# The queue that issues the stores of the gated output: Pool's in place of SyncE's

## The chip, the cores and the metric

The program runs on one core of a Trainium2 chip. The metric is the device time of one execution in microseconds, as the median of several. Before the change three executions took 2771.98, 2772.40 and 2774.57 us, so the median is 2772.4 us.

The engines are named as in the profile: PE is TensorE's matmul and PEld its weight load, DVE is VectorE, ACT is ScalarE, POOL is GpSimd and SP is SyncE, which in this kernel does nothing but issue DMAs. SPq is SP's queue of such issues.

## The reference, cut to what matters

One layer (DEPTH = 1) of a backbone with width 1024 works on 2048 latent tokens and 128 context tokens: a bidirectional gated recurrence (HGRN2), then a feed-forward block with a short convolution, then a final norm. The change touches the feed-forward block alone:

```python
def conv_ffn(h, w_up, conv_w, conv_b, w_down, grid_axis):
    a, g = jnp.split(h @ w_up, 2, axis=-1)
    a = token_conv(a, conv_w, conv_b, grid_axis)
    return (jax.nn.silu(a) * g) @ w_down
...
xp = xp + mod_p[5] * conv_ffn(hp, ffn_w_up[l], ffn_conv_w[l], ffn_conv_b[l], ffn_w_down[l], None)
xs = xs + mod_s[5] * conv_ffn(hs, ffn_w_up[l], ffn_conv_w[l], ffn_conv_b[l], ffn_w_down[l], 2)
```

The inner width (D_FF) is 2816, so `h @ w_up` gives 5632 columns: 2816 for `a`, which is convolved over three neighbours in a row of 64 latent tokens (or in the 128 context tokens), and 2816 for the gate `g`.

## The kernel before

**Operands.** Every f32 operand of a matmul is kept as two f16 tiles, a high part and a remainder, and a product is three matmuls (high by high, high by low, low by high). The high part is written by ACT and the remainder by DVE (`split`, L970 and L971; for weights `part`, L1037 and L1038 in the up stage, L1232 and L1233 in the down stage).

**Pieces.** The latent tokens go in four pieces of 512 (p = 0 to 3), the context is a fifth piece (CTX) of 128. The 2816 inner columns are 22 blocks of 128 and are taken two at a time (`cb` = 0, 2, ..., 20), so there are 11 periods of the up stage. One period makes, for p = 0 to 3, `up(cb, p)`, and after p = 1 also `up_ctx(cb)` for the context.

**Up stage.** A product of a 2x2 block of weights with a 2x2 block of tokens takes seven partial products (Strassen and Winograd's scheme) in the order 1, 2, 6, 5, 7, 3, 4. `product` issues twelve matmuls for one of them into a bank (L1076) and evacuates it: by ACT where it writes a quarter of the result (L1085, L1089, L1091, L1097), by DVE where it adds to one (L1082). Two such sets run side by side, one for `a` and one for `g`.

**Weights of the up stage.** `quad(cb, i)` loads the raw f32 weights `r` of two column blocks (L1043, two loads of 512 KB; i = 0 for `a`, i = 1 for `g`), forms the four sums `s` on DVE (L1048 to L1051) and splits the eight operands into `w` (L1037 and L1038). The two quads of the next period are put on a list (`pending`) after `up_ctx`, and steps of them are handed out between products (`post`).

**Gated output.** When `up(cb, p)` has its result, `gate(cb, p)` is put on another list: it convolves `a` (ACT L1103, DVE L1110 and L1112), applies silu (ACT L1137), multiplies by the gate (DVE L1139), forms the four sums `t` of the tokens' quarters (DVE L1147 to L1151), and splits all seven operands of the down stage into the tile `u` (L970 and L971). `u` is then stored to DRAM, in `UD[p]` (L1158): 896 KB, 1792 rows of 512 B, once for each of 11 x 4 latent pieces. `gate_ctx` does the same for the 128 context tokens without sums and stores 64 KB into `UC` (L1191), 22 times.

**Down stage.** `load_rd` brings raw weights `rawd` (L1228, 704 KB each), `part` splits them into `wd`, `sums_down` makes sums of them (L1244 to L1248), `load_uc` and `load_ut` read the stored outputs back as `U` (L1270, L1289), `load_xd` the residual `x` (L1264). `down_ctx` multiplies for the context (L416 to L418, added to `x` at L1283), `down` for the latent pieces (L1307, added at L1316). `final_norm` ends a piece; its power function is on Pool (L344). The first loads of `rawd` and their splitting fall into the last period of the up stage.

**Order.** The code states what each engine does; a scheduler puts the instructions of each engine into a fixed order at build time, with the help of its own estimate of durations, and each engine then runs them in order and waits where an operand isn't ready. Before the change every DMA of the kernel is issued by SP, in one order. Tiles live in SBUF at places given out by `place`, which reuses the place of a tile whose last reader has come: a load into a tile waits for whatever still reads what lay there before, and a store is such a reader until it has landed.

Of the kernel before, what the change touches and what calls it, by code (L numbers as in the profile page):

```python
# [214 lines left out]
def stages(nc, tl, pt, drt, xT, adaH, adaT, pvec, w_in, w_out, w_up, w_down, state, yT, st_out):  # L215
# [752 lines left out]
    def split(dst, src, scale=None):  # L968

        A.activation(dst[0], src, AF.Copy)  # L970
        V.tensor_tensor(dst[1], src, dst[0], ALU.subtract)  # L971
# [127 lines left out]
    def conv(cols, p, n):  # L1099


        for cb, y, a in cols:
            A.activation(y, a, AF.Identity, bias=pv[:, PV_CB + cb : PV_CB + cb + 1],  # L1103
                         scale=cws[:, 22 + cb : 23 + cb])
        yield
        row = ROW if p != CTX else n
        for cb, y, a in cols:
            y3 = y.rearrange("p (r c) -> p r c", c=row)
            a3 = a.rearrange("p (r c) -> p r c", c=row)
            V.scalar_tensor_tensor(y3[:, :, 1:], a3[:, :, : row - 1], cws[:, cb : cb + 1],  # L1110
                                   y3[:, :, 1:], ALU.mult, ALU.add)
            V.scalar_tensor_tensor(y3[:, :, : row - 1], a3[:, :, 1:], cws[:, 44 + cb : 45 + cb],  # L1112
                                   y3[:, :, : row - 1], ALU.mult, ALU.add)
        yield
# [4 lines left out]
    UD = {p: drt([P, 7, 2, NCB // 2, HN], F16, f"ud{p}") for p in range(CTX)}  # L1119
    UC = drt([P, NCB, 2, NCTX], F16, "uc")  # L1120
# [11 lines left out]
    def gate(cb, p, qa, qg):  # L1132
        y = tl([P, 2, 2, HN], F32, "y")
        flat = y.rearrange("p j h c -> p (j h c)")
        yield from conv([(cb + j, flat[:, 512 * j : 512 * j + 512], qa["out"][j])
                         for j in range(2)], p, 512)
        A.activation(flat, flat, AF.Silu)  # L1137
        yield
        V.tensor_tensor(flat, flat, qg["tile"], ALU.mult)  # L1139
        yield  # L1140
        u = tl([P, 7, 2, HN], F16, "u")

        def part(z, src):
            split((u[:, z : z + 2, 0], u[:, z : z + 2, 1]), src)

        t13 = tl([P, 2, HN], F32, "t")
        V.tensor_tensor(t13[:, 0], y[:, 0, 1], y[:, 0, 0], ALU.subtract)  # L1147
        V.tensor_tensor(t13[:, 1], y[:, 1, 1], y[:, 0, 1], ALU.subtract)
        t24 = tl([P, 2, HN], F32, "t")
        V.tensor_tensor(t24[:, 0], y[:, 1, 1], t13[:, 0], ALU.subtract)  # L1150
        V.tensor_tensor(t24[:, 1], y[:, 1, 0], t24[:, 0], ALU.subtract)  # L1151
        part(0, y[:, :, 0])
        split((u[:, 6, 0], u[:, 6, 1]), y[:, 1, 1])
        yield
        part(2, t13)
        yield
        part(4, t24)
        nc.sync.dma_start(UD[p][:, :, :, cb // 2], u)  # L1158

    def up(cb, p):  # L1160
        qs = []
        for i, s in enumerate((1.0, IWS)):
            t = tl([P, 2 * 512], F32, "c7")
            qs.append({"scale": s, "tile": t,
                       "out": [t[:, 512 * j : 512 * j + 512] for j in range(2)]})
        for i in (1, 2, 6, 5, 7, 3, 4):
            while any(PROD[i][0] not in WQ.get((cb, j), {}) for j in range(2)):
                post()
            for j in range(2):
                product(qs[j], i, WQ[cb, j], TT[p])  # L1170
            post()
            tick()
            if i == 6 and cb + 2 == NCB and p + 1 == CTX:
                load_uc()
                load_ut(0, "B11")
                for j in range(2):
                    load_xd(CTX, j, 0, NCTX)
                load_xd(0, 0, 0)
        gates.append(gate(cb, p, *qs))

    def gate_ctx(cb, a, g):
        n = NCTX
        y = tl([P, n], F32, "y")
        yield from conv([(cb, y, a)], CTX, n)
        A.activation(y, y, AF.Silu)
        yield
        V.tensor_tensor(y, y, g, ALU.mult)
        u = tl([P, 2, n], F16, "u")
        yield
        split((u[:, 0], u[:, 1]), y)  # L1190
        nc.sync.dma_start(UC[:, cb], u)  # L1191

    def up_ctx(cb):
        n = NCTX
        for j in range(2):
            pa, pg = pt([P, 512], "pj"), pt([P, 512], "pj")
            for pp, i in ((pa, 0), (pg, 1)):
                for k in range(KT):
                    wt = WQ[cb, i][("A11", "A12", "A21", "A22")[2 * j + k // 4]]
                    ks = slice(k % 4 * P, k % 4 * P + P)  # L1200
                    mm3(pp[:, :n], (wt[:, 0, ks], wt[:, 1, ks]), TT[CTX][:, :, k], n,
                        k == 0, k == KT - 1)
            a, g = tl([P, n], F32, "y"), tl([P, n], F32, "y")
            A.activation(a, pa[:, :n], AF.Copy)
            A.activation(g, pg[:, :n], AF.Copy, scale=IWS)
            pending.append(gate_ctx(cb + j, a, g))
            post()
# [268 lines left out]
```

## Time and profile before

| | before |
|---|---|
| median of three executions | 2772.4 us |
| the profiled execution | 2777.14 us |
| its span on the core | 2775.2 us |
| mean granted clock of TensorE | 0.993 |
| the up stage's periods in the trace | about 1430 to 2325 us |
| ud stores (L1158) | 44 of 896 KB, median 4.8 us from issue to landing |
| uc stores (L1191) | 22 of 64 KB, median 1.5 us |
| r loads (L1043) | 44 of 512 KB, median 4.0 us |
| rawd loads (L1228) | 20 of 704 KB, median 8.1 us |
| U loads from ud (L1289) | 56 of 704 KB, median 4.9 us |

The span runs from the first to the last instruction in the trace. The time of the profiled execution is 1.9 us longer than that, and 4.7 us above the median. In the rows of the profile an instruction has its engine, its line in the kernel, its operation and its tiles, written as out<-in. In a timeline the start comes first and the duration second; the bracket at the end tells how long the engine idled before it, and what ended this. In a table of waits a row has the engine and the line that waited, what it waited for, and then the sum in us, the number of waits and the longest one.

### The profile page before, as it was taken

The page shows a single profiled execution, that of the slowest core. Times are in us where ns is not written, and L with a number is a line of the kernel's source. Part 1 is how long each engine was busy: PE and PEld are TensorE (multiplying, and loading weights), DVE is VectorE, ACT ScalarE, POOL GpSimd, SP SyncE. Part 2 cuts the span into 40 slices and gives each one's busy share as a digit, 9 for nine tenths or more (in the row PEclk, how much of TensorE's full clock was granted, in tenths as well). Part 3 has the DMA queues.
Part 4 walks back from the last instruction along what each step waited for, and adds up shares of the span by engine and source line. Part 5 has one row for each costly group of instructions (what it writes and reads, how often), then busy time and mean ns, then how long its engine had stood idle before and what let it go on. Part 6 is the DMA issues. An engine that isn't in the chain of part 4 may idle for free.

```text
span 2775.2 us, 57195 instructions
## 1 busy us (share of the span) xinstructions
PE 2705.4 (97%) x23576; PEld 2129.1 (77%) x23576; DVE 1886.0 (68%) x5324; ACT 1071.8 (39%) x2373; POOL 72.9 (3%) x84
## 2 busy tenths in 40 slices
PE   8999999999999999999999999999999999999998
PEld 4677777777777677765578888888888988888887
DVE  7887887887876766755996767666677677623123
ACT  5533334343434242513664545445455453300000
POOL 0100000000000000000000000000000000000000
PEclk9999999999999999999999999999999999999999
DMA  7011213121201010345112232221212275344352
GB/s 265 27 63 42 70 34 95 32 74 39 73 6 54 6 54 4 110 137 194 67 41 85 63 89 67 73 86 56 86 58 77 77 200 170 127 156 137 123 166 73
DMA packets 194005, 239.73 MB, mean 86 GB/s; under 512 B 12368, under 2 KB 148432, under 8 KB 193744
## 3 DMA queue, kind: packets, MB, share of 16 engines
q1 hardware_dynamic: 193744, 236.08, 26.9%
q8 instruction: 185, 3.03, 0.5%
q14 instruction: 76, 0.62, 0.1%
HBM read 166.44 MB, written 69.60 MB: 85 GB/s over the span
## 4 chain that ended last, share of the span: by engine, by line
PE 58%; DVE 16%; DMA 5%; ACT 2%; issue 2%; POOL 0%; SPq 0%; DVEq 0%; POOLq 0%; ACTq 0%
PE pj_p L1307 11%; PE pj_p L1076 9%; PE sc_p L1076 6%; PE pj_p L418 5%; PE pj_p L416 5%; PE pj_p L417 5%; DMA r<-w_up 3%; PE pj_p L539 3%; PE pj_p L538 3%; PE pj_p L540 3%; DMA ud<-u 2%; DVE u L971 2%; PE sc_p L1307 1%; PE sc_p L692 1%; DVE wd L1233 1%
## 5 line engine op out<-in xcount | busy, mean ns | idle before, releaser
L1076 PEld LDWEIGHTS <-w 128*128 128x128 f16 x7392 | 725.0, 98 | 115.4 <-issue 29.7
L1076 PE MATMUL pj_p<-T,w 128*128 128x256 f16 x4224 | 491.0, 274 | 24.2 <-DVE c L1082 16.4
L1307 PEld LDWEIGHTS <-wd 128*128 128x128 f16 x3696 | 361.5, 98 | 53.5 <-issue 8.8
L1076 PE MATMUL sc_p<-T,w 128*128 128x256 f16 x3168 | 367.8, 273 | 0.0
L1307 PE MATMUL pj_p<-U,wd 128*128 128x256 f16 x3168 | 354.3, 273 | 5.7 <-DVE x L1316 5.7
L416 PE MATMUL pj_p<-H,wp 128*128 128x512 f16 x768 | 291.2, 380 | 2.8 <-ACT H L395 2.4
L417 PE MATMUL pj_p<-H,wp 128*128 128x512 f16 x768 | 292.6, 381 | 0.5 <-DVE H L400 0.4
L418 PE MATMUL pj_p<-H,wp 128*128 128x512 f16 x768 | 292.3, 381 | 0.0
L540 PE MATMUL pj_p<-wp,H 128*128 128x256 f16 x1024 | 279.1, 273 | 0.0
L538 PE MATMUL pj_p<-wp,H 128*128 128x256 f16 x1024 | 279.1, 273 | 0.0
L539 PE MATMUL pj_p<-wp,H 128*128 128x256 f16 x1024 | 279.1, 273 | 0.0
L1316 DVE SCALAR_TENSOR_TENSOR x<-pj_p,g,x 128x256 f32<-128x256 f32 x96 | 46.4, 483 | 211.6 <-PE pj_p L1307 211.5
L418 PEld LDWEIGHTS <-wp 128*128 128x128 f16 x960 | 94.2, 98 | 91.4 <-issue 2.6
L416 PEld LDWEIGHTS <-wp 128*128 128x128 f16 x960 | 94.3, 98 | 83.5 <-issue 4.2
L417 PEld LDWEIGHTS <-wp 128*128 128x128 f16 x960 | 94.2, 98 | 81.1 <-issue 2.0
L363 ACT ACTIVATE n<-x 128x256 f32<-128x256 f32 (+1 forms) x63 | 25.0, 403 | 262.9 <-DVE x L1316 201.9
L1103 ACT ACTIVATE y<-c,pv,cws 128x512 f32<-128x512 f32 x88 | 71.2, 811 | 137.1 <-DVE c L1082 133.9
L511 ACT ACTIVATE f<-pj_p 128x512 f32<-128x512 f32 x64 | 38.0, 596 | 185.2 <-PE pj_p L418 185.1
L539 PEld LDWEIGHTS <-H 128*128 128x128 f16 x1024 | 100.2, 98 | 11.8
L540 PEld LDWEIGHTS <-H 128*128 128x128 f16 x1024 | 100.2, 98 | 11.7
L538 PEld LDWEIGHTS <-H 128*128 128x128 f16 x1024 | 100.3, 98 | 11.5
L417 PE MATMUL pj_p<-og,wo 128*128 128x512 f16 (+1 forms) x320 | 108.9, 349 | 0.0
(281 smaller groups left out, 5037.6 us busy)
## 6 DMA issues: line engine op xcount, KB each, us to landing
ud<-u SPq DMA_DIRECT2D x44, 896.0 KB, 4.8
U<-ud SPq DMA_DIRECT2D x56, 704.0 KB, 4.9
r<-w_up SPq DMA_DIRECT2D x44, 512.0 KB, 4.0
wr<-w_in SPq DMA_DIRECT2D x40, 512.0 KB, 4.2
wr<-adaT SPq DMA_DIRECT2D x32, 512.0 KB, 3.7
rawd<-w_down SPq DMA_DIRECT2D x20, 704.0 KB, 8.1
x<-xT SPq DMA_DIRECT2D x32, 256.0 KB, 5.3
sp<-oT SPq DMA_DIRECT2D x32, 256.0 KB, 2.2
```

The source lines that it names most:

```text
L416: T.matmul(out, whl[0], hhl[:, 0, :n], start=first, stop=False)
L417: T.matmul(out, whl[0], hhl[:, 1, :n], start=False, stop=False)
L418: T.matmul(out, whl[1], hhl[:, 0, :n], start=False, stop=last)
L511: A.activation(ft, pj[:, :n], AF.Tanh, scale=0.5 * IWS)
L538: T.matmul(o, hp[k][:, 0, tok], wvg[0][:, k], start=(k == 0), stop=False)
L539: T.matmul(o, hp[k][:, 0, tok], wvg[1][:, k], start=False, stop=False)
L540: T.matmul(o, hp[k][:, 1, tok], wvg[0][:, k], start=False, stop=(k == KT - 1))
L971: V.tensor_tensor(dst[1], src, dst[0], ALU.subtract)
L1076: T.matmul(out, wt[:, a, ks], tt[:, b, k], start=first and k == 0 and n == 0, stop=i in (2, 3, 4) and k == 3 and n == 2, skip_group_check= ...
L1103: A.activation(y, a, AF.Identity, bias=pv[:, PV_CB + cb : PV_CB + cb + 1], scale=cws[:, 22 + cb : 23 + cb])
L1307: T.matmul(out, w[:, a, k], UT[p, zb][b][:, k], start=first and i % 2 == 0 and k == 0 and q == 0, stop=n in (2, 3, 4) and k == KP - 1 and ...
L1316: V.scalar_tensor_tensor(x, get(src), g64[:, 1, m, 0:1], x, ALU.mult, ALU.add)
```

## The change

The two stores of the gated output are issued by Pool's queue instead of SP's. Nothing else in the code differs:

```diff
@@ gate @@
         part(4, t24)
-        nc.sync.dma_start(UD[p][:, :, :, cb // 2], u)
+        nc.gpsimd.dma_start(UD[p][:, :, :, cb // 2], u)
...
@@ gate_ctx @@
         split((u[:, 0], u[:, 1]), y)
-        nc.sync.dma_start(UC[:, cb], u)
+        nc.gpsimd.dma_start(UC[:, cb], u)
```

SP then has 489 rows in its program in place of 555, and Pool 155 in place of 89. Loads stay with SP. The tiles keep their places in SBUF. As the scheduler's estimate changes with the queue, some instructions of DVE and ACT change places too; the rows below show it at three places, `-` for before and `+` for the change. In a row stand the line, the operation, out<-in with the numbers of the tiles, and the shape.

SP in the up stage, from the first period on: between loads of raw weights (`r`) stood the stores of a gated latent piece (`ud`) and of the gated context (`uc`).

```order
 L1043 DMA r_18298<-w_up 128x1024
-L1158 DMA ud_15452<-u_17998 1792x1x256
 L1043 DMA r_18300<-w_up 128x1024
-L1191 DMA uc<-u_18187 128x256
-L1191 DMA uc<-u_18257 128x256
-L1158 DMA ud_15453<-u_18284 1792x1x256
 L1043 DMA r_18478<-w_up 128x1024
 L1043 DMA r_18480<-w_up 128x1024
-L1158 DMA ud_15454<-u_18622 1792x1x256
-L1158 DMA ud_15455<-u_18843 1792x1x256
 L1043 DMA r_19358<-w_up 128x1024
```

The loads keep their order and follow one another; the same stores stand in Pool's program in the same order, after the last of its small instructions for the norms (L344) and with nothing between them.

DVE in one of the periods of the up stage, when the second quad of the next period comes in: `r_22718` and `r_22720` are its two raw blocks, `s_...` the four sums, `c_2572` and `c_2573` the results that are being evacuated from the banks `pj` and `sc`.

```order
+L1050 TENSOR_TENSOR s_22724<-r_22718,r_22720 128x512
 L1048 TENSOR_TENSOR s_22722<-r_22720 128x512
+L1049 TENSOR_TENSOR s_22723<-s_22722,r_22718 128x512
+L1051 TENSOR_TENSOR s_22725<-r_22718,s_22723 128x512
 L1082 SCALAR_TENSOR_TENSOR c_2572_22428<-pj_p_22430,c_2572_22428 128x256
-L1049 TENSOR_TENSOR s_22723<-s_22722,r_22718 128x512
-L1050 TENSOR_TENSOR s_22724<-r_22718,r_22720 128x512
 L1082 SCALAR_TENSOR_TENSOR c_2573_22429<-pj_p_22444,c_2573_22429 128x256
-L1051 TENSOR_TENSOR s_22725<-r_22718,s_22723 128x512
 L1082 SCALAR_TENSOR_TENSOR c_2572_22428<-sc_p_22550,c_2572_22428 128x256
```

One sum stood ahead of the first evacuation, now all four do. The same holds in four more periods, with the quads 20598, 23778, 24838 and 25898, where two, three, one and three sums stood ahead of it.

ACT in the last period, where the up stage goes over into the down stage: `wd_...` are the high parts of the down weights made from `rawd_...`, `c_2944` and `c_2945` results of the up stage's last products but one, and `u_28881` a context store's tile.

```order
+L1232 ACTIVATE wd_28925<-rawd_28453 128x1408
 L1085 ACTIVATE c_2945_28813<-pj_p_28828 128x256
 L970 ACTIVATE u_28881<-y_28846 128x128
+L1232 ACTIVATE wd_28993<-rawd_28796 128x1408
 L1089 ACTIVATE c_2944_28812<-pj_p_28814 128x256
-L1232 ACTIVATE wd_28925<-rawd_28453 128x1408
+L1232 ACTIVATE wd_28996<-rawd_28798 128x1408
 L1089 ACTIVATE c_2945_28813<-pj_p_28828 128x256
+L1232 ACTIVATE wd_28922<-rawd_28451 128x1408
 L1091 ACTIVATE c_2944_28812<-sc_p_28928 128x256
-L1232 ACTIVATE wd_28993<-rawd_28796 128x1408
-L1232 ACTIVATE wd_28922<-rawd_28451 128x1408
```

Three of the splittings L1232 stand one to three places earlier than before: `wd_28925` ahead of an L1085, `wd_28993` (into the place that the `u` of piece 1 has left) and `wd_28996` ahead of an L1089.

## The prediction

> **What bounds the kernel now.** I begin with the page: the shares of the engines, then a table by stretches of time for the part of the program that the stores stand in, then PE's waits in it.
>
> ```profile
> PE 2705.4 (97%) x23576; PEld 2129.1 (77%) x23576; DVE 1886.0 (68%) x5324; ACT 1071.8 (39%) x2373; POOL 72.9 (3%) x84
> 1430.00:2250.00 820.00, 799.72 (x7723) 716.71 (x7721) 573.10 (x1101) 410.58 (x872) 0.00 (x0) 1.00 0.27 78
> 2250.00:2330.00 80.00, 71.76 (x817) 65.39 (x815) 68.42 (x91) 39.26 (x61) 0.00 (x0) 0.94 0.70 204
> ```
>
> The last two rows give, for a stretch, its length and the busy time of PE, PEld, DVE, ACT and POOL, then granted clock, DMA share and GB/s. PE is the bound. In the up stage it idles for 820.00 − 799.72 = 20.3 us, and in the 80 us in which the up stage goes over into the down stage for 80.00 − 71.76 = 8.2 us. The DMA engines are 27% busy and POOL does nothing at all, so neither is short of time; a store matters only where somebody waits for it, or for a load behind it. The waits in the up stage:
>
> ```profile
> PE pj_p L1076 <- DVE c L1082: 15.5, 13, 2.6
> PE pj_p L1076 <- ACT c L1085: 2.4, 6, 0.6
> PE pj_p L1076 <- ACT c L1089: 1.1, 1, 1.1
> PE pj_p L1076 <- ACT y L1204: 1.0, 4, 0.4
> SPq L1043 <- DMA ud<-u: 62.3, 15, 4.4
> ACT w L1037 <- DMA r<-w_up: 59.5, 14, 7.2
> DVE s L1048 <- DMA r<-w_up: 33.1, 8, 5.0
> ```
>
> PE is never held by a DMA itself, only by evacuations on DVE and ACT that stand in order behind an instruction which waits for a load of raw weights `r`. And 15 times such a load was itself waiting for a **store to land** (the SPq row), because the tile `r` takes memory that a `u` still being stored holds. SP is idle then: its order costs nothing at these places, only the store's landing does. One of them, on SP, ACT and PE:
>
> ```profile
> 1754.99 0.51 SPq L1158 DMA_DIRECT2D ud<-u  x1
> 1759.85 1.85 SPq L1043 DMA_DIRECT2D r<-w_up  x2
> 1764.15 0.63 ACT L1037 ACTIVATE w<-r 128x512 f16<-128x512 f32 x1 [6.48 <-DMA r<-w_up]
> 1770.65 0.49 PE L1076 MATMUL pj_p<-T,w 128*128 128x256 f16 x3 [0.18 <-ACT y L1204]
> ```
>
> The store begins at 1754.99; 4.86 us later the load starts, 4.3 us after that ACT, and ACT's later work holds PE for 0.18 us. Whatever the store lands later, PE waits longer.
>
> **The change, term by term.** 44 stores of 896 KB and 22 of 64 KB leave SP's queue for Pool's. SP issues 66 instructions fewer, which by itself saves nothing, as SP has slack. Pool has none of its own work in the up stage. The bytes stay, the tiles and their memory stay.
>
> ```profile
> L1158 SPq DMA_DIRECT2D ud<-u x44: 513/519/767, 1445.0 to 2342.2; - x44
> DMA to landing us min/median/max: 4.8/4.8/6.8
> L344 POOL TENSOR_TENSOR rs<-rs,mh 128x4 f32<-128x4 f32 (+2 forms) x19 | 21.7, 1144 | 1567.6 <-DVE rs L342 1567.6
> ```
>
> *Unknown price Δ: how much later than now a store lands if Pool issues it.* No DMA of the trace is issued by Pool. Lower end: Pool is as prompt as SP, Δ = 0 (0.52 us for the issue, 4.8 to the landing); nothing shows a store that undercuts 4.8, so I don't go below. Upper end: the slowest landing of these stores, 6.8 − 4.8 = +2.0. A near row is the smallest work that Pool does, 1.144 us for 128x4 numbers against SP's 0.52, +0.6. I take the middle of +0.6 and +2.0, **Δ = +1.3**, since a store of 1792 rows is more than that instruction. (The Trainium skill, "DMA: Bandwidth & Descriptors", section "Latency and other measured facts", gives a first byte after about 1 us from Pool and 0.6 from SP; an estimate of Δ = +0.4 by that page would make the next term +3.2 and the whole sum −3.8. No run here shows it.)
>
> *Loads that wait for a landing.* Of the 15, followed to PE one by one, 8 end in a wait of PE (0.18 to 1.14 us now, at 1477.5, 1509.6, 1521.3, 1545.5, 1609.3, 1770.6, 1937.5, 2100.4); these have no slack, and pay Δ in full. Three more of them:
>
> ```profile
> 1477.53 2.67 PE L1076 MATMUL pj_p<-T,w 128*128 128x256 f16 x23 [1.14 <-ACT c L1089]
> 1520.26 0.69 DVE L1050 TENSOR_TENSOR s<-r,r 128x512 f32<-128x512 f32 x1 [4.02 <-DMA ud<-u]
> 2100.42 0.49 PE L1076 MATMUL pj_p<-T,w 128*128 128x256 f16 x3 [0.26 <-ACT y L1204]
> 1657.54 0.51 SPq L1158 DMA_DIRECT2D ud<-u  x1
> 1662.37 0.34 SPq L1043 DMA_DIRECT2D r<-w_up  x1
> 1665.75 4.53 PE L1076 MATMUL pj_p<-T,w 128*128 128x256 f16 x40
> 1670.12 2.78 PE L1076 MATMUL sc_p<-T,w 128*128 128x256 f16 x24
> ```
>
> The other 7 are like that of 1662.37: the load waits too, but PE runs on without a gap; they have some 1.5 to 2 us of slack by the same following. Term: 8 × 1.3 = **+10.4** (0 to +16 between the ends).
>
> *Loads that stand behind a store in SP's queue.* In five periods the last `r` of the next block's weights is issued right behind a store, and shares the queue with it:
>
> ```profile
> 1780.40 0.52 SPq L1158 DMA_DIRECT2D ud<-u  x1
> 1781.33 1.74 SPq L1043 DMA_DIRECT2D r<-w_up  x1
> r<-w_up SPq DMA_DIRECT2D x1, 512.0 KB, 3.7
> r<-w_up SPq DMA_DIRECT2D x1, 512.0 KB, 7.3
> 1788.76 0.69 DVE L1048 TENSOR_TENSOR s<-r 128x512 f32<-128x512 f32 x1 [5.04 <-DMA r<-w_up]
> 1789.37 0.42 DVE L1082 SCALAR_TENSOR_TENSOR c<-pj_p,c 128x256 f32<-128x256 f32 x1
> 1789.84 5.41 PE L1076 MATMUL pj_p<-T,w 128*128 128x256 f16 x32 [2.63 <-DVE c L1082]
> ```
>
> The `r` ahead of the store lands in 3.7 us, the one behind it in 7.3 (the two DMA rows, of the windows 1779:1781 and 1781:1790), and PE loses 2.63 us. With the store in another queue the second should land between 3.7 and 7.3 us after its issue: 0 to 3.6 us earlier, I take the middle, 1.8. But the new program order on DVE takes half of it back. Of the four sums (0.61 us from start to start: 1788.76 to 1789.37) more stand ahead of the evacuation L1082 than before: 4 instead of 2, 1, 3, 1 and 3 in the five periods, 10 more in all, 6.1 us. Term: 6.1 − 5 × 1.8 = **−3** (from 6.1 − 18 = −12 to +6). That PE waits longer than 2.6 us here also halves its clock for a moment (32 matmuls in 5.41 us above, where 48 take 5.40 elsewhere: 1.8 us); that goes or stays with the wait, inside these ends.
>
> *The transition.* Here SP really holds the stores up, behind loads whose issue is slow:
>
> ```profile
> 2252.43 15.61 SPq L1228 DMA_DIRECT2D rawd<-w_down  x6
> 2268.13 2.36 SPq L1191 DMA_DIRECT2D uc<-u  x1
> 2270.60 0.52 SPq L1158 DMA_DIRECT2D ud<-u  x1
> 2263.76 0.68 DVE L971 TENSOR_TENSOR u<-t,u 128x512 f16<-128x512 f32 x1
> 2274.22 1.38 ACT L1232 ACTIVATE wd<-rawd 128x1408 f16<-128x1408 f32 x1 [6.04 <-DMA uc<-u]
> 2275.63 1.63 DVE L1233 SCALAR_TENSOR_TENSOR wd<-rawd,wd 128x1408 f16<-128x1408 f32 x1 [6.38 <-ACT wd L1232]
> PE pj_p L1076 <- ACT c L1089: 2.9, 1, 2.9
> PE pj_p L418 <- DVE wd L1233: 3.7, 1, 3.7
> ```
>
> The `u` was whole at 2264.44 (end of the DVE row), its store left at 2270.60. Pool would issue it some 6 us sooner, beside loads that fill the DMA engines. ACT waits 6.04 and DVE 6.38 us; of the shortfall PE pays 2.9 us at once and 1.6 + 3.7 us at 2321 to 2327, when DVE has been full since 2275. Against it stands ACT's new order: the L1232 that reuses the large `u` now comes ahead of the L1089 that PE needs. It waits for a landing at 2264.4 + 4.8 + Δ = 2270.5 if nothing hinders it, 6 us later if the loads do (now it lands in 6.0). Term: the best is all of 2.9 + 5.3 and as much again of halved clock, about −14; the worst is L1089 3 us later than now, +3. I take **−4**, as the loads still fill the engines there.
>
> **Sum**: 10.4 − 3 − 4 = +3.4 us. The profiled execution took 2777.1 us (span 2775.2), 4.7 over the median 2772.4; +3.4 makes 2780.5 of it, or **2776** against the median. After the up stage I count nothing: the last store leaves at 2342 and POOL's next instruction comes at 2356.3.
>
> **Rivals.** *A: Pool is slow with 1792 rows.* If writing the packets' list takes Pool longer than the engines take to move them, Δ goes past 2. Against it: POOL's L344 does its work in 1.1 us. For it: the 1792 rows of 512 B are many, and SP already takes 0.52 us instead of the 0.33 of an `r`. From Δ = 2 the other 7 places lose their slack too, and waits of PE over 2.6 us cost 1.8 us of clock each. At Δ = 2.5: 8 × 2.5 + 7 × 0.7 + 8 × 1.8 − 7 = +32, **2805**; at 4.5 (the delay that an uc store, 1.5 us, has at worst, 6.0): 36 + 19 + 15 − 7 = +63, 2835. A related mechanism is that a busy DVE (573.10 of 820 us) holds Pool's writing of that list up, by an instruction at a time; its price is bounded by the two above. The Trainium skill, "SBUF — State Buffer", section "Who interferes with whom", has that for copies, casts and tensor-by-scalar operations of DVE, not for two-tensor ones; the DVE rows above are all of two tensors, so by that page this does not happen here.
>
> ```profile
> DMA to landing us min/median/max: 1.5/1.5/6.0
> ```
>
> *B: the gains win.* Δ at most 0.3: 8 × 0.2 = +1.6, the second `r` lands 2.5 us sooner (6.1 − 12.5 = −6) and the transition gives −7: −11, **2761**. For it: 7.3 against 3.7 us, and 6 us of queueing that the rows show. Against it: DVE's and ACT's new orders.
>
> *C: nothing moves.* The stores use the same 16 engines, and if they are served in the same turn, all landings stay; the new orders then cost and bring about nothing: **2772**.
>
> **How the numbers follow.** The forecast (Δ from 0.6 to 2, sum −8 to +18) has a chance of 0.47: 0.08 faster, 0.25 same, 0.14 slower, each by over 0.2% (5.5 us, about what a measurement of this kernel can tell from none). A 0.25, all slower. B 0.18, all faster. C 0.10, same. Together faster 0.26, same 0.35, slower 0.39. The forecast's own range is 2764 to 2790; the whole range takes in B and most of A, 2758 to 2825.
>
> **What would show it.** The landing of L1158 in the changed profile gives Δ: near 6.1 for the forecast, 4.8 for B, over 6.8 for A. The gaps at the eight places should each have grown by Δ; the second `r` should land in under 7.3 us, yet DVE's L1082 start about as late as now; the 6.04 and 6.38 us waits at 2268 to 2276 should be shorter. Wrong would be: ud landings under 4.8 us, `r` loads slowed by sharing the engines with a store at places that have no store behind them now, or a PE gap at the places with slack.

## The result, and the profile after

The changed kernel takes 2807.85 us (median of 4, 2806.36 to 2810.33) against 2773.49 us for the kernel before, run beside it: a ratio of 1.0124 with a 95% interval of 1.0111 to 1.0137, so 34.4 us slower. The profiled execution took 2810.33 us with a span of 2808.3, against 2777.14 and 2775.2 before.

From the page of the changed kernel, the engines, the new queue beside the old one, and the landing times:

```profile
PE 2717.3 (97%) x23576; PEld 2134.5 (76%) x23576; DVE 1889.3 (67%) x5324; ACT 1072.3 (38%) x2373; POOL 131.4 (5%) x150
q1 hardware_dynamic: 111024, 194.26, 21.0%
q0 software_dynamic: 11264, 41.82, 4.8%
ud<-u POOLq DMA_DIRECT2D x44, 896.0 KB, 5.5
r<-w_up SPq DMA_DIRECT2D x44, 512.0 KB, 3.6
```

POOL's busy time grew by the 66 issues, and queue q0 now carries their bytes. PE does the same 23576 matmuls, yet is busy 2717.3 − 2705.4 = 11.9 us longer. That is time at a lower clock: the stretches in which the granted clock is 0.5 add up to 64.0 us in this trace and to 40.8 in that of before, and half of the difference is 11.6 us. So of the 33 us in the span about a third is clock and two thirds are waits. The waits of PE in the up stage (from 1430 to 2300 us), and those that the stores end:

```profile
PE pj_p L1076 <- DVE c L1082: 29.6, 11, 5.0
PE pj_p L1076 <- ACT c L1085: 6.5, 10, 2.2
PE pj_p L1076 <- ACT y L1204: 2.6, 4, 0.8
PE pj_p L1076 <- ACT c L1089: 0.3, 1, 0.3
  DVE s L1048: 5.0, 5
  DVE s L1050: 4.7, 1
DMA to landing us min/median/max: 5.4/5.5/9.6
```

The first row has doubled (15.5 before), and its longest wait is 5.0 instead of 2.6. The two DVE rows are from the view of line L1158, which says who waited for its stores: DVE's sums L1048 now do, five times; before they did not appear there at all. The landings have a median of 5.5 us from Pool's start and a longest of 9.6, against 4.8 and 6.8.

**Where in the program.** The start of every 168th matmul of L1076 marks a piece, 44 in the up stage, four to a period. (In the trace of before these matmuls run from 1396.1 to 2302.8 us, not from about 1430 to 2325, as the table of times at the start has it.) Cutting both traces there, and adding up what the pieces of a kind take longer than before, gives this (us; worked out from the matmul rows of the profiled executions, which themselves differ by several us between executions of one kernel):

```
                 periods 1-9,      periods 1-9,      period 10   after the last   all, to PE's
                 pieces 0 and 1    pieces 2 and 3                L1076            last matmul
after                +4.7              +22.5            +3.5          +1.9           +32.9
p1_pool              +1.5              +19.4            +3.1          -0.1           +23.3
p1_sp                +5.2               +5.0            +1.9          +3.2           +13.0
p1_act               -0.1               +9.4            +1.1          +0.3           +10.2
order_pool           +4.9               +7.9            +2.7          +3.3           +19.0
late_pool            +6.4              -17.7            +2.7          +2.5            -6.3
late_sp              -0.5              -18.9            +1.3          +1.0           -18.1
uc_pool              -1.3               -5.0            +1.3          -1.2            -6.3
last_pool            -1.4               -3.6            +2.3          +4.4            +1.1
```

The last column also holds what lies ahead of period 1. The row of uc_pool, whose median is that of the kernel before, shows how far one trace can be off: −5.0 in one column. Part of that is clock: the trace of before has two stretches of 3.41 us at half clock in these pieces, each a loss of 1.7 us, and that of uc_pool has none. So differences of a few us in the table decide nothing. The loads that wait for a landing (pieces 0 and 1) cost little. Two thirds of the loss sit in pieces 2 and 3, nearly all of it in piece 2, where the second quad of the next block comes in. One such place, in period 6. Before, from the timelines of SP, DVE and PE:

```profile
1947.26 0.52 SPq L1158 DMA_DIRECT2D ud<-u  x1
1948.20 0.35 SPq L1043 DMA_DIRECT2D r<-w_up  x1
1954.94 0.69 DVE L1048 TENSOR_TENSOR s<-r 128x512 f32<-128x512 f32 x1 [4.36 <-DMA r<-w_up]
1955.55 0.42 DVE L1082 SCALAR_TENSOR_TENSOR c<-pj_p,c 128x256 f32<-128x256 f32 x1
1956.02 5.62 PE L1076 MATMUL pj_p<-T,w 128*128 128x256 f16 x48 [1.95 <-DVE c L1082]
```

After, from those of SP, POOL, DVE and PE:

```profile
1960.37 2.16 SPq L1043 DMA_DIRECT2D r<-w_up  x2
1961.78 1.06 POOL L1158 DMA_DIRECT2D ud<-u  x1 [1.85 <-DVE u L971]
1968.02 0.69 DVE L1050 TENSOR_TENSOR s<-r,r 128x512 f32<-128x512 f32 x1 [3.44 <-issue]
1970.15 0.69 DVE L1048 TENSOR_TENSOR s<-r 128x512 f32<-128x512 f32 x1 [1.43 <-DMA ud<-u]
1972.21 0.75 DVE L1082 SCALAR_TENSOR_TENSOR c<-pj_p,c 128x256 f32<-128x256 f32 x2
1972.68 8.30 PE L1076 MATMUL pj_p<-T,w 128*128 128x256 f16 x48 [4.61 <-DVE c L1082]
```

Read these from below. PE waits 4.61 us instead of 1.95 and then runs its 48 matmuls in 8.30 us, which take 5.40 at full clock. It waited for an evacuation L1082, which stood on DVE behind four sums instead of one. The first of them, L1050, needs both raw blocks, and they are there by 1968.0 (the second lands at 1967.94). The next, L1048, could start at once if it only needed `r`; it waits 1.43 us more **for the store to land**, because its tile `s` takes the memory of the `u` that is being stored. It lands at 1970.12. The sum needed the landing before too: there the store stood ahead of the load in SP's queue and landed at 1953.61, the load at 1954.86, so the load's landing hid it, and the profile put the wait down to the load alone. It is the same in all five periods in which DVE's order changed: before, the store landed 1.2 to 2.3 us ahead of the second load; after, it lands 1.5 to 2.2 us behind it (from the landings in the two traces).

### The profile page after: what moved, and what is told of

It reads as the page before. It is cut to its first block, busy times and chain, and to the rows that moved or that the text cites. A ratio compares the mean times of both kernels' runs of the same rounds, so it can differ in the third digit from the quotient of the medians.

```text
span 2808.3 us, 57270 instructions
## 1 busy us (share of the span) xinstructions
PE 2717.3 (97%) x23576; PEld 2134.5 (76%) x23576; DVE 1889.3 (67%) x5324; ACT 1072.3 (38%) x2373; POOL 131.4 (5%) x150
## 3 DMA queue, kind: packets, MB, share of 16 engines
q1 hardware_dynamic: 111024, 194.26, 21.0%
q0 software_dynamic: 11264, 41.82, 4.8%
## 4 chain that ended last, share of the span: by engine, by line
PE 42%; issue 28%; DVE 9%; DMA 2%; POOL 2%; ACT 1%; POOLq 0%; SPq 0%; DVEq 0%; ACTq 0%
PE pj_p L1307 11%; PE pj_p L418 5%; PE pj_p L416 5%; PE pj_p L417 5%; PE pj_p L539 3%; PE pj_p L538 3%; PE pj_p L540 3%; DMA ud<-u 1%; PE sc_p L1307 1%; PE sc_p L692 1%; POOL ud L1158 1%; PE sc_p L652 1%; PE sc_p L661 1%; DVE x L1330 1%; DVE T L971 1%
## 5 line engine op out<-in xcount | busy, mean ns | idle before, releaser
L1076 PEld LDWEIGHTS <-w 128*128 128x128 f16 x7392 | 730.0, 99 | 141.7 <-issue 50.9
L1076 PE MATMUL pj_p<-T,w 128*128 128x256 f16 x4224 | 499.9, 277 | 44.6 <-DVE c L1082 30.5
L1076 PE MATMUL sc_p<-T,w 128*128 128x256 f16 x3168 | 369.1, 273 | 0.1
```

The costliest lines, as they stand in the source:

```text
L1076: T.matmul(out, wt[:, a, ks], tt[:, b, k], start=first and k == 0 and n == 0, stop=i in (2, 3, 4) and k == 3 and n == 2, skip_group_check= ...
```

## The experiments

All times are medians, beside runs of the kernel before on the same chip (2773.2 us with the first four, 2773.3 with the others). The first three are about which stores bring the loss, and which queue.

**Piece 1's stores alone on Pool** (p1_pool):

```diff
-        nc.sync.dma_start(UD[p][:, :, :, cb // 2], u)
+        (nc.gpsimd if p == 1 else nc.sync).dma_start(UD[p][:, :, :, cb // 2], u)
```

> Only the stores of piece 1 (11 of 44) go to Pool, all else stays with SP. Theory 1: the loss sits where the sums s (or raw blocks r) of the next block's second quad take the memory of the piece-1 output that is still being stored, and the evacuations L1082 stand behind those sums on DVE; then nearly all of the 34 us is here: 2772 + 22 to 26, so 2794 to 2798 us, with the third piece of most periods 1 to 5 us longer than before. Theory 2 (every Pool store pays about 1.2 us where a load waits for its landing, as the forecast had it): the first pairs wait for piece-0 stores, which stay with SP, so 2770 to 2776.

It took 2798.55 us, a ratio of 1.0091 (1.0068 to 1.0114). Eleven of the 66 stores bring 25 us, almost all in pieces 2 and 3. In the same trace, the two kinds of stores land side by side (issues by queue), and DVE's sums wait for them (from the view of line L1158):

```profile
ud<-u SPq DMA_DIRECT2D x33, 896.0 KB, 4.8
ud<-u POOLq DMA_DIRECT2D x11, 896.0 KB, 7.8
  DVE s L1048: 8.7, 6
```

That is half a microsecond above the range of theory 1, which is right about these stores. The forecast's reading, that they cost next to nothing, is not.

**All others on Pool, piece 1 on SP** (p1_sp): the same line with `p == 1` going to `nc.sync` and the rest to `nc.gpsimd`, and the context stores on Pool.

> The counterpart: the stores of pieces 0, 2, 3 and of the context go to Pool, piece 1 stays with SP. Theory 1: what is left is the first pairs, 0.3 to 0.6 us each and 2.5 once, 5 to 9 us in all: 2777 to 2782. Theory 2: eight places at 1.2 us and the odd ones in part: 2782 to 2800.

It took 2790.06 us, 1.0057 (1.0038 to 1.0076): 17 us, more than theory 1 allowed and inside the range of theory 2. The table shows it spread out: 5 us at the loads that wait for a landing, 5 in pieces 2 and 3, 2 in period 10 and 3 at the end. The table's numbers are near what one trace can be off, so this spread is rough. Some of it is clock: at one place in period 2 a wait of PE grew from 2.02 to 2.69 us, and the 48 matmuls behind it took 7.07 us, where 48 take 5.40 at full clock.

```profile
1628.13 7.07 PE L1076 MATMUL pj_p<-T,w 128*128 128x256 f16 x48 [2.69 <-DVE c L1082]
```

The two parts add up to 42 us where the whole change cost 34, so they aren't independent.

**Piece 1's stores on ACT's queue** (p1_act): the line of p1_pool with `nc.scalar` in place of `nc.gpsimd`. In the five periods DVE's order comes out as in the change.

> Piece-1 stores go to ACT's queue: a queue of their own, but not Pool's; DVE's order comes out as in the change (all four sums ahead of the evacuations). Theory 1a (a separate queue: store and raw load share the engines, the store lands last, and the sum waits for it): most of the loss stays, 2785 to 2795. Theory 1b (Pool is slow to bring a store out): the loss goes, 2770 to 2778.

It took 2782.44 us, 1.0031 (1.0017 to 1.0046), 9 us, between the two theories. (Its ten executions spread from 2774.59 to 2787.95, and the profiled one, 2787.33, is among the slowest; by the interval the loss is 5 to 13 us.) In period 6 the store is now out before the second load, and the load decides again, as before; all four sums still stand ahead of L1082:

```profile
1951.06 0.52 ACTq L1158 DMA_DIRECT2D ud<-u  x1
1958.14 0.69 DVE L1050 TENSOR_TENSOR s<-r,r 128x512 f32<-128x512 f32 x1 [3.78 <-DMA r<-w_up]
```

In the five periods the store now lands 0.2 to 1.3 us behind the second load, in p1_pool 1.5 to 2.9. Of the 25 us of p1_pool, then, some 9 come with a separate queue, as ACT's is, and DVE's new order, and some 16 with Pool's.

**The sums behind the evacuations, all stores on Pool** (late_pool). A scheduling hint without a semaphore makes each of the four sums of a second quad follow, on DVE, the last L1082 written out so far; the lines left out only bring in what the hint needs.

```diff
+        def late(op):
+            if op is not None and i == 1 and cb > 0:
+                CTXT[0].add_manual_dep(op.ins, LAST[0].ins.name, ONLY, reason="order")
...
-        V.tensor_tensor(s1, a21, a22, ALU.add)
+        late(V.tensor_tensor(s1, a21, a22, ALU.add))
...
-            V.scalar_tensor_tensor(dst, src, sc, dst, ALU.mult, ALU.add)
+            LAST[0] = V.scalar_tensor_tensor(dst, src, sc, dst, ALU.mult, ALU.add)
```

> The change, with the four sums of each block's second quad put behind the evacuations L1082 in DVE's order; all stores stay with Pool. Theory 1: the late landing then holds up only the sums, which have slack; the third pieces lose their waits, those of before too (24.7 us of loss, some 14 us of old waits and the halved clock after them): 2755 to 2772. Rival (the loss comes from loads of r that share the engines with Pool's stores, wherever the sums stand): 2795 to 2808.

It took 2771.92 us, 0.9996 (0.9987 to 1.0005): with every store still on Pool, the time is that of the kernel before again. (The hint takes away waits that the kernel before had, too; its counterpart without Pool is late_sp, below.) PE's waits in the up stage:

```profile
PE pj_p L1076 <- ACT c L1085: 11.3, 11, 3.8
PE pj_p L1076 <- ACT y L1204: 3.3, 5, 1.0
PE pj_p L1076 <- DVE c L1082: 3.3, 4, 1.9
```

The row of L1082 falls from 29.6 to 3.3 us. The loss by the rival, loads slowed by sharing the engines, would have stayed. What remains is mostly the L1085 row, at the first pairs and in the last period.

**Pool's stores with DVE's old order** (order_pool): the same hint, but each sum of the five second quads whose order the change had moved is tied to the L1082 that it used to follow; a 0 in the list leaves the sum free.

```diff
+        def late(z, op, n={6: {1: 0, 2: 1, 3: 0, 4: 1}, 10: {1: 0, 2: 1, 3: 1, 4: 2}, 12: {1: 0, 2: 0, 3: 0, 4: 1}, 14: {1: 0, 2: 1, 3: 1, 4: 2}, 16: {1: 0, 2: 0, 3: 0, 4: 1}}):
+            if op is not None and i == 1 and n.get(cb, {}).get(z):
+                CTXT[0].add_manual_dep(op.ins, LAST[n[cb][z] - 5].ins.name, ONLY, reason="order")
```

> The change with all its Pool stores, but in the five periods DVE's sums and evacuations L1082 stand as before the change. Theory A (the late landing of the piece-1 store is the cause, the order only adds what the three extra sums take): 1.2, 1.8, 0.6, 1.8 and 0.6 us come back, with some of the halved clock: 2808 less 6 to 14, so 2794 to 2802 us. Theory B (the order of the sums is the cause): nearly all of the third pieces' loss comes back, 2775 to 2786.

It took 2802.67 us, 1.0103 (1.0087 to 1.0118), 5 us under the change and just above the range of theory A; its profiled execution, at 2796.28, was its fastest, so its row in the table shows too small a loss. Theory B is out. The place of period 6, on DVE, and the line's waits:

```profile
1959.85 0.69 DVE L1048 TENSOR_TENSOR s<-r 128x512 f32<-128x512 f32 x1 [5.59 <-DMA ud<-u]
1960.46 0.41 DVE L1082 SCALAR_TENSOR_TENSOR c<-pj_p,c 128x256 f32<-128x256 f32 x1
  DVE s L1048: 12.7, 5
```

With the old order the one sum ahead of L1082 waits for the store itself.

**The kernel before with late sums** (late_sp): the diff of late_pool on the kernel before, all stores by SP.

> The kernel before (all stores by SP), with the four sums of the second quad behind the evacuations as in late_pool. If the waits of PE behind L1082 (some 14 us, and 1.8 us of halved clock at five of them) are DVE's order alone: 2745 to 2758 us, faster than both kernels. If they only move to the next instruction that waits for r: 2765 to 2773.

It took 2757.54 us, 0.9943 (0.9929 to 0.9958): 16 us under the kernel before and 50 under the change, the fastest of all. In the up stage PE's wait for L1082 fell from 15.5 to 1.9 us, and little came in its place:

```profile
PE pj_p L1076 <- DVE c L1082: 1.9, 3, 1.1
1430.00:2250.00 820.00, 814.17 (x7953) 733.61 (x7952) 589.65 (x1130) 423.22 (x894) 0.00 (x0) 1.00 0.29 84
```

PE is idle 5.8 of these 820 us, where it was 20.3. Against late_pool it is also the measure of what Pool costs where no sum stands in the way: 2771.92 − 2757.54 = 14 us, close to the 17 of p1_sp. With the sums ahead of the evacuations the same stores cost 34 us. So some 20 of the 34 reach PE through these sums. The table agrees: in pieces 2 and 3 the rows of late_pool and late_sp differ by 1.2 us, those of the change and the kernel before by 22.5.

**Context stores alone on Pool** (uc_pool): only the line L1191 is changed.

> Only the 22 context stores of 64 KB go to Pool. No load of the up stage waits long for them: 2769 to 2777 us, the same as before. If two of them cost what a piece-1 store costs: 2785 or more.

2773.79 us, 1.0005 (0.9996 to 1.0014): no difference.

**The last block's stores alone on Pool** (last_pool): both lines choose `nc.gpsimd` for `cb + 2 == NCB` (the context's for `cb >= NCB - 2`).

> Only the stores of the last block (four of 896 KB, two of 64 KB) go to Pool, with ACT's and DVE's order of the transition as in the change. The forecast's term for the transition was -4: 2768 us. By the changed profile the third piece of the last period, its first and the end after it are 2.8, 0.5 and 1.9 us longer: 2775 to 2779.

2779.49 us, 1.0019 (1.0008 to 1.0031): 6 us slower, half a microsecond above what the changed profile had led to, and not the forecast's gain. The transition in the changed kernel, on POOL, ACT and PE:

```profile
2293.01 0.55 POOL L1191 DMA_DIRECT2D uc<-u  x1 [12.20 <-DVE u L971]
2295.27 1.05 POOL L1158 DMA_DIRECT2D ud<-u  x1 [1.70 <-ACT wd L1232]
2299.04 1.38 ACT L1232 ACTIVATE wd<-rawd 128x1408 f16<-128x1408 f32 x1 [3.50 <-DMA uc<-u]
2300.32 0.37 ACT L1085 ACTIVATE c<-pj_p 128x256 f32<-128x256 f32 x1
2303.72 1.38 ACT L1232 ACTIVATE wd<-rawd 128x1408 f16<-128x1408 f32 x1 [2.83 <-DMA ud<-u]
2300.74 2.72 PE L1076 MATMUL pj_p<-T,w 128*128 128x256 f16 x12 [3.88 <-ACT c L1085]
```

Pool does issue the stores at once, but the engines are full of `rawd` loads (300 GB/s from 2285 to 2304 us): the 64 KB of `uc` land only when ACT goes on at 2299.0, 6.0 us after the issue. ACT's waits of 3.50 and 2.83 us add up to about what its one wait was before (6.04), and since the L1232 now stands ahead of an L1085, PE waits 3.88 us where it waited 2.92.

## Why the prediction was right or wrong

**Direction and range.** A slower kernel was the likeliest of the three outcomes, with a chance of 0.39, and 2807.85 lies within 2758 to 2825. That is luck more than insight: the forecast's own range ended at 2790, and the range reached further only for rival A, whose mechanism is not what the runs show. The likeliest case, 2776, was wrong: +3.4 us was forecast, 34 came.

**What bounds the kernel** held: PE waits only for evacuations, and those stand behind something that waits for a DMA.

**Δ** was right for a store that has the engines to itself, and too small for those that cost most. At the place that the prediction showed (store at 1754.99, load at 1759.85, 4.86 us), the changed trace has:

```profile
1763.88 1.29 DVE L971 TENSOR_TENSOR u<-t,u 128x512 f16<-128x512 f32 x2
1765.46 1.04 POOL L1158 DMA_DIRECT2D ud<-u  x1 [17.21 <-DVE u L971]
1771.20 0.83 SPq L1043 DMA_DIRECT2D r<-w_up  x2
1774.76 0.63 ACT L1037 ACTIVATE w<-r 128x512 f16<-128x512 f32 x1 [6.89 <-DMA r<-w_up]
1781.27 0.60 PE L1076 MATMUL pj_p<-T,w 128*128 128x256 f16 x4 [0.59 <-ACT y L1204]
```

The `u` is whole at 1765.17, Pool starts 0.29 us later, and the load starts 6.03 us after the `u`; before it was 4.88 (the same row of DVE ended at 1754.97, and the store left SP 0.02 us later). So Δ is 1.1 us, where 1.3 was taken. The estimate from the first-byte times of the Trainium skill ("DMA: Bandwidth & Descriptors", section "Latency and other measured facts") was +0.4, too little here: Pool's issue (1.04 against 0.51) and its later start (0.29 against 0.02) alone differ by 0.8. Piece 1's stores, which run beside raw loads, are another matter. They landed in a median of 6.0 us after their `u` was whole, and land in 8.4 now, so their Δ is 2.4. The prediction took one Δ for all stores.

**Loads that wait for a landing: +10.4 forecast, about +5 measured** (pieces 0 and 1 in the table). The places were right, the price was mis-sized: PE's gap at this one grew from 0.18 to 0.59, not by 1.1. ACT went on 3.56 us after the load's start instead of 4.30, as the load itself was faster; that gave 0.7 us back.

**Loads that stand behind a store in SP's queue: −3 forecast (−12 to +6), about +22 measured.** This is the step that failed. It held that "the second should land between 3.7 and 7.3 us after its issue" and counted what an earlier landing gives and what the extra sums take. The loads did land sooner: in the five periods in 6.0 us after their issue, the mean, instead of 7.0. But the step looked at the load only, since the wait was put down to it, and never asked what else the sum waits for. The prediction's own rows held the sign: the sum at 1520.26 waits for `ud<-u` itself, and was counted among the loads. The sum writes into the memory of a `u` whose store SP's order had put ahead of the load. In a queue of its own that store lands last: 7.8 us after Pool's start in p1_pool, where it shares the engines with raw loads, against a median of 5.5 for all stores in the change. Late_pool and late_sp show that this is how the loss reaches PE (some 20 us go when the sums stand back), order_pool that the landing matters with the old order too, and p1_act that the new order with another queue is about a third of p1_pool's loss. In period 6 the slower clock adds 8.30 − 5.40 = 2.9 us to the wait of 4.61.

**The transition: −4 forecast, about +3.5 measured** (period 10 in the table; the +6 of last_pool also holds what comes after it). The prediction had both sides, stores out sooner and ACT's order worse, and had set its worst end at +3. Wrong was how much sooner the stores land with the engines full: the `ud` store left only 0.75 us after its `u` was whole, where it had waited 6.2, but took 8.4 us to land instead of 6.0. The prediction's "6 us later if the loads do" does not follow from the row it names; a landing in 6.0 us is 1.2 later than one in 4.8.

**After the up stage: nothing forecast, about +2 measured**; in late_pool, too, the end is 2.5 us longer, in last_pool 4.4. Which of the two last stores does it was not tried.

**The rivals.** Rival A's time, 2805, is near the result, but not for its reason. It needed a Δ of 2.5 at every store because Pool is slow with the rows; Δ is 1.1 at the place above and 2.4 only beside raw loads, where ACT's queue, too, landed the stores late (7.3 us after its start). And A's reckoning has no instruction on DVE that itself waits for a landing. Its side mechanism, DVE holding up Pool's writing of descriptors, isn't needed for what was seen; Pool's issue took 1.04 to 1.21 us everywhere. Its price for waits over 2.6 us isn't a rule either, as the last section shows. B's gains were there (stores leave sooner, loads land sooner) and lost to the in-order engines behind. C is out: landings did move.

**What stays open.** In p1_sp the second raw load of period 2 lands some 0.6 us later than before although its own store is on SP, and no run tells why.

## What to carry to other kernels

A wait in a profile names only what came last. Before a transfer is moved to another queue, look for what the waiting instruction needs besides, memory that is still being stored above all, because the old queue's order may have been what made that free. And an instruction that waits for a load should not stand, on an in-order engine, ahead of evacuations that need nothing: moving four sums of each period took 16 us off the kernel before, and no choice of queue tried here gained anything.

## What the runs showed of the hardware

Pool's queue moved 41.82 MB in 11264 packets, 3.7 KB each. SP's q1 lost 193744 − 111024 = 82720 packets with those bytes, 506 B each. The same rows of 512 B are thus packed differently by the two queues. The landing was not faster for it (a median of 5.5 us against 4.8).

Raw loads land in a median of 3.6 us instead of 4.0 when all stores are in Pool's queue, even where the store had landed before the load was issued (3.48 against 4.22 us at 1771.20 and 1759.85). Why is not shown; SP's two issues there took 0.83 us in all instead of 1.85.

After some of PE's waits the granted clock is 0.5 for 3.41 us, which costs 1.7 us. The length of the wait alone did not decide it. Before, a wait of 2.02 us at 1872.5 was followed by such a stretch, and one of 2.02 at 1627.85 was not; in p1_act one of 1.95 was, and in late_pool one of 3.79 was not.
